# Three edits to a two-layer streaming encoder kernel: an enforced order of the out-projection's products, a sum's base load on GpSimd's queue, and the final norm's buffers in the tiles of the X sums

## The chip, the cores and the metric

The kernel runs on one core of a Trainium2 chip. A core has a matrix engine (TensorE, PE in the rows; its weight loads are PEld), a vector engine (VectorE, DVE), a scalar engine (ScalarE, ACT), a general engine (GpSimd, POOL) and SyncE (SP), which here only issues transfers. Each engine works through its own queue in order and waits there for semaphores of the others. SP and GpSimd both issue loads from the chip's memory; loads that add to what is already in the tile are issued by GpSimd here. The metric is the device time of one execution in microseconds (us), the median of several runs.

## The reference

One inference step of a two-layer encoder on 640 frames (512 of a new stream, 8 x 16 of running streams), with 1024 features, in float32:

```
def swiglu_ffn(h, g, w_in, w_out):
    a, b = jnp.split(rms_norm(h, g) @ w_in, 2, axis=-1)
    return h + (jax.nn.silu(a) * b) @ w_out
...
for l in range(DEPTH):          # DEPTH = 2
    if l < N_A_LAYERS:          # layer 0
        h, st = conv_module(h, conv_hist[l], ...)
    else:                       # layer 1
        h = h + o @ w_o[j]      # o: chunked band attention over a shared K and V
    h = swiglu_ffn(h, norm_ffn[l], w_ffn_in[l], w_ffn_out[l])
return rms_norm(h, norm_final), jnp.stack(new_hist, axis=0), k, v
```

The hidden width of the FFN is 2816, so w_in is 1024 x 5632 and w_out 2816 x 1024. The change lies in the two FFNs and in the last line's norm.

## The kernel before

The residual stream `h` stays on the chip as 8 tiles of 128 features by 640 frames. A float32 product is made of three TensorE products of split operands: each operand is cut into a high part (ACT copies it, rounded) and a low part (DVE subtracts the high one), and high x high, low x high and high x low are summed in one bank of PSUM. `cut` does this for weights (line 319 for ACT, 320 for DVE), `product` (line 383) issues the three matmuls of each 128-row step.

**The FFN** multiplies blocks in the manner of Strassen: the 640 frames are halved into 2 x 320 columns and the contraction into two halves, and seven products of sums replace eight plain ones. The sums of the normed input are kept for the whole FFN in tiles `XH0` to `XH6` and `XL0` to `XL6` (high and low parts of X11, X21, XT2, XT1, XT3, XT4, X22). The weight side needs its own sums for each block; `w_seven` makes them. It loads the block of four quarters into one of two `raw` tiles and the third quarter into one of two sum tiles `s1`, both from SP, and then adds the fourth quarter to `s1` with an adding load from GpSimd (line 365). DVE makes the other sums (lines 369, 370, 372), and each of the seven goes through `cut` into one of eleven weight slots that are used in turn: a slot is free when TensorE has done the product eleven places before.

The in-projection runs over 22 tiles of hidden features, 18 of them in three chunks of six. `seven` issues the products of one such tile (84 matmuls); the last two of them are handed on as `after(0)` and `after(1)` and issued within the next tile. Their sinks make the gated hidden values and their Strassen sums, again as high and low parts (tiles `hid`).

After each chunk `out_chunk` adds the chunk's part of the out-projection: four blocks u = 0 to 3, seven products each (63 matmuls), each product followed by an add of its PSUM bank to `h` on DVE (line 512). `QORD` names the order: the first digit is the product (5 XT1, 1 X11, 2 X21, 6 XT2, 3 X22, 7 XT3, 4 XT4), the second the block, and a0 and a1 are the last in-projection tile's `after(0)` and `after(1)`. The hidden sums of that tile come out of a0 and a1 alone, so the third 128-row step of products 6, 3, 7 and 4 can't begin before a1's residue is through ACT and DVE. The program is written in this order, but the order on each engine is set by a scheduler that weighs priorities against a timeline of its own; it may place matmuls of several products between one another, as long as the data allow it.

The last four hidden tiles are handled without block sums: `mm3` (lines 167 to 169) multiplies them by w_out for all 8 output tiles, first for frames 256 to 639, then for frames 0 to 255, and DVE adds each result to `h` (line 621).

**The final norm** follows for the same two groups of frames, g = 1 (384 frames) and g = 0 (256). `rstd_bc` squares the 8 tiles of `h` on ACT (line 175), sums the squares on DVE (line 194), takes the mean over partitions on TensorE (line 203), adds epsilon on DVE (line 237), raises to -0.5 on GpSimd (line 244) and spreads the result over the partitions on TensorE (line 215). Then the tiles of `h` are scaled, for g = 1 four on DVE (line 1216) and four on ACT and GpSimd (lines 1219, 1221), for g = 0 all on DVE, and stored from SP. The squares go through a new pool `tp3` with two tiles, and the sum and the copy `b1` of the spread lie in that pool too.

## Time and profile before

| | us |
| --- | --- |
| median of 3 runs | 1525.98 (1524.56 to 1526.48) |
| profiled execution | 1530.94 |
| its span, first to last instruction | 1528.9 |
| mean granted TensorE clock | 0.980 of full speed |

The first FFN lies at about 255 to 672 us of the span, the second at about 1048 to 1505 us, the final norm behind it. Times in rows are us from the span's start, durations of one instruction in ns or us as said there. In the rows a name stands for a tile, `out<-in`; buffer numbers are left out, so `s` is a sum tile `s1`, `w` the PSUM tile of a norm, `whi`, `wlo`, `shi` and `slo` weight slots. A bracket at the end of a timeline row gives how long the engine sat idle before it and what ended that. A matmul's end is modelled, so two matmuls that follow each other without a pause overlap in the rows; how full TensorE is, is better read from the number of matmuls in a stretch.

### The profile page before, as it was taken

The numbers are of one execution on the slowest core, as the hardware profiler recorded it, in microseconds if no ns is written. First come the engines' busy times: TensorE is split into PE (matmuls) and PEld (weight loads), VectorE is DVE, ScalarE is ACT, GpSimd is POOL, SyncE is SP. The second block draws the span as 40 slices with busy tenths as digits, with TensorE's granted clock in tenths as the row PEclk, the third lists the DMA queues.
The fourth block names the chain that finished last, engine by engine and source line by source line (L and its number), as shares of the span: only waits on it lengthen the run. The fifth ranks groups of instructions, "written<-read, shape, count | busy, mean of one in ns | idle before, by whom it ended". The sixth has DMA issues, their size and how long they took to land.

```text
span 1528.9 us, 28150 instructions
## 1 busy us (share of the span) xinstructions
PE 1456.1 (95%) x10974; PEld 1378.4 (90%) x10974; DVE 1120.0 (73%) x2481; ACT 746.7 (49%) x1617; POOL 281.8 (18%) x312
## 2 busy tenths in 40 slices
PE   5999899999999999999999999988999999999995
PEld 5998689999999999999887888957999999999994
DVE  5789346798888887856676667653799788688844
ACT  3666245464554563545554454442465464464432
POOL 5789232000000000013221121011000001001001
PEclk9999889999999999999999999988999999999997
DMA  7267414134444444424555455551124543444501
GB/s 236 65 185 182 102 48 132 44 101 117 149 116 126 139 116 132 111 83 149 193 188 189 138 173 187 168 166 42 56 76 111 158 127 93 143 138 92 169 29 69
DMA packets 71013, 192.57 MB, mean 126 GB/s; under 512 B 12000, under 2 KB 33248, under 8 KB 62432
## 3 DMA queue, kind: packets, MB, share of 16 engines
q1 hardware_dynamic: 61664, 175.78, 35.7%
q0 software_dynamic: 8928, 14.68, 6.4%
q8 instruction: 86, 1.41, 0.4%
q10 hardware_dynamic: 288, 0.31, 0.1%
q14 instruction: 47, 0.39, 0.1%
HBM read 179.14 MB, written 11.61 MB: 125 GB/s over the span
## 4 chain that ended last, share of the span: by engine, by line
PE 77%; DVE 8%; POOL 5%; DMA 5%; ACT 3%; issue 2%; SPq 0%; POOLq 0%; DVEq 0%; ACTq 0%
PE mm L383 44%; PE mm L167 7%; PE mm L168 7%; PE mm L169 7%; POOL ca L730 4%; PE mm L768 2%; DMA raw<-in_w_in 1%; PE w L1105 1%; PE w L203 1%; PE am L1090 1%; DVE wlo L320 1%; DMA cache<-in_ck 1%; PE am L1073 1%; PE am L1136 1%; DMA s<-in_w_in 1%
## 5 line engine op out<-in xcount | busy, mean ns | idle before, releaser
L383 PE MATMUL mm<-XH,whi 128*128 128x320 f32 x896 | 275.8, 310 | 4.5 <-DVE t L397 3.0
L383 PE MATMUL mm<-XH,wlo 128*128 128x320 f32 x896 | 276.5, 310 | 0.0
L383 PE MATMUL mm<-XL,whi 128*128 128x320 f32 x896 | 273.8, 309 | 0.0
L319 ACT ACTIVATE whi<-raw 128x512 fp32r<-128x512 f32 (+2 forms) x280 | 166.3, 612 | 156.7 <-PE mm L383 90.5
L167 PE MATMUL mm<-xh,whi 128*128 128x320 f32 (+2 forms) x640 | 202.0, 317 | 4.6 <-ACT xh L156 2.6
L168 PE MATMUL mm<-xh,wlo 128*128 128x320 f32 (+2 forms) x640 | 201.2, 315 | 0.6 <-DVE wlo L151 0.6
L169 PE MATMUL mm<-xl,whi 128*128 128x320 f32 (+2 forms) x640 | 198.1, 314 | 0.0
L320 DVE TENSOR_TENSOR wlo<-raw,whi 128x512 fp32r<-128x512 f32 (+2 forms) x280 | 183.6, 670 | 14.1 <-ACT whi L319 12.7
L383 PE MATMUL mm<-hid,whi 128*128 128x320 f32 x732 | 172.2, 309 | 2.6 <-ACT whi L319 2.3
L383 PEld LDWEIGHTS mm<-XH,whi 128*128 128x128 f32 x896 | 167.8, 188 | 6.5 <-DVE t L397 3.5
L383 PEld LDWEIGHTS mm<-XH,wlo 128*128 128x128 f32 x896 | 168.2, 188 | 0.5 <-DVE wlo L320 0.5
L383 PEld LDWEIGHTS mm<-XL,whi 128*128 128x128 f32 x896 | 167.6, 188 | 0.0
L167 PEld LDWEIGHTS mm<-xh,whi 128*128 128x128 f32 x640 | 122.5, 192 | 8.1 <-ACT xh L156 3.1
L383 PEld LDWEIGHTS mm<-hid,whi 128*128 128x128 f32 x732 | 124.9, 188 | 4.0 <-ACT whi L319 3.4
L365 POOL DMA_DIRECT2D s<-in_w_in x38 | 33.8, 890 | 503.9 <-DVE XL L320 115.7
L168 PEld LDWEIGHTS mm<-xh,wlo 128*128 128x128 f32 x640 | 122.7, 192 | 1.2 <-DVE wlo L151 0.8
L169 PEld LDWEIGHTS mm<-xl,whi 128*128 128x128 f32 x640 | 121.5, 191 | 1.2 <-issue 1.0
L383 PE MATMUL mm<-hid,wlo 128*128 128x320 f32 x366 | 112.5, 308 | 0.0
L383 PE MATMUL mm<-XL,shi 128*128 128x320 f32 x344 | 105.4, 308 | 1.3 <-DVE XL L320 1.3
L383 PE MATMUL mm<-XH,shi 128*128 128x320 f32 x344 | 106.0, 308 | 0.4 <-ACT XH L319 0.4
L383 PE MATMUL mm<-XH,slo 128*128 128x320 f32 x344 | 106.0, 308 | 0.1
L319 ACT ACTIVATE shi<-raw 128x512 fp32r<-128x512 f32 (+1 forms) x114 | 66.4, 587 | 73.5 <-PE mm L383 38.6
(229 smaller groups left out, 3368.7 us busy)
## 6 DMA issues: line engine op xcount, KB each, us to landing
raw<-in_w_in SPq DMA_DIRECT2D x38, 1024.0 KB
raw<-in_w_os SPq DMA_DIRECT2D x24, 768.0 KB
cache<-in_ck SPq DMA_DIRECT2D x32, 512.0 KB
cache<-in_cv SPq DMA_DIRECT2D x32, 512.0 KB
raw<-in_w_pw SPq DMA_DIRECT2D x12, 1024.0 KB
s<-in_w_in SPq DMA_DIRECT2D x38, 256.0 KB
s<-in_w_in POOLq DMA_DIRECT2D x38, 256.0 KB, 4.8
raw<-in_w_kq SPq DMA_DIRECT2D x8, 1024.0 KB
```

Of the source, the lines that this page charges most:

```text
L167: nc.tensor.matmul(ps, wh, xh, start=(i == 0), stop=False)
L168: nc.tensor.matmul(ps, wl, xh, start=False, stop=False)
L169: nc.tensor.matmul(ps, wh, xl, start=False, stop=(i == last))
L203: nc.tensor.matmul(st[:, 512 + t * w + k:513 + t * w + k], s[:, a:a + P], onec, start=True, stop=True)
L319: nc.scalar.activation(out=hi, in_=src, func=AF.Copy)
L320: nc.vector.tensor_tensor(out=lo, in0=src, in1=hi.bitcast(F32), op=sub)
L365: nc.gpsimd.dma_start(s1, src[:, 3 * n:4 * n], accum_op=add)
L383: nc.tensor.matmul(pt, wt, v, start=(first and k == i == 0), stop=(k == len(xs) - 1 and i == 2), skip_group_check=True)
L730: nc.gpsimd.tensor_tensor(out=acc, in0=acc, in1=pr, op=ALU.add)
L768: nc.tensor.matmul(pt[32 * q:32 * q + 32, 0:n], w4[0:r, 4 * tg + q, :], mv, start=(tg == 0), stop=(tg == 7))
L1073: nc.tensor.transpose(tr[:, o:o + P], S[:, SOFF[i] + k * P:SOFF[i] + (k + 1) * P], ident)
L1090: nc.tensor.matmul(po[r, k * P:512], VT[:, 1 + k, v0:v0 + DH], PTs[hh][:, POFF[k]:POFF[k] + n], start=(k == 0), stop=(k == 3))
```

## The change

Three edits:

1. In `out_chunk` each product is issued after the last matmul of the one named before it in `QORD` (`issue_after`), a0 and a1 included. This binds the scheduler's order and puts no wait into the program, since all of it is on one engine. Products 60 and 30 are written in two parts: the first two 128-row steps (60', 30') and the third (60", 30").
2. In `w_seven` the base of the sum tile, the third quarter, is loaded from GpSimd's queue instead of SP's, at the priority of the adding load.
3. The final norm's squares, sums and `b1` get no pool of their own. `ffn` hands back `spare`, which takes the tiles `XH0` to `XH6` again: for g = 1 the squares and the sum lie in XH0 to XH2 and `b1` in XH3, for g = 0 in XH4 to XH6.

```diff
@@ -58,7 +58,8 @@
 X11, X21, XT2, XT1, XT3, XT4, X22 = range(7)
 NCH, CW = 3, 6
 HIX = {X11: 0, X21: 1, XT1: 2, XT2: 3, XT3: 4, X22: 5, XT4: 6}
-QORD = "50 a0 10 a1 20 51 11 60 30 21 70 61 31 40 52 71 12 22 41 62 32 53 72 13 23 42 63 33"
+QORD = """50 a0 10 a1 20 60' 30' 51 60" 11 30" 70 21 61 40 31 52 71 12 22 41 62 32 53 72 13 23 42 63
+          33"""
 BO = "a0 s0 a1 s1 b0 b1 t0 p0 c0 t1 c1"
 BL = "a0 s0 a1 s1 t0 b0 b1 c0 t1 c1 p0"
 SSQ1 = 'ppapappp'
@@ -231,7 +232,7 @@
                 accp=None, sqs=None):
         st = w2t()
         nt = len(tiles(n))
-        r, v = colmean(st, [lambda s=s, e=e, i=i: square(s, n, e, sqs if sqs is None else sqs[:, i, :])
+        r, v = colmean(st, [lambda s=s, e=e, i=i: square(s, n, e, sqs and sqs[i])
                          for i, (s, e) in enumerate(zip(pieces, engs))], n,
                        cut, "rst", eng, accp)
         nc.vector.tensor_scalar(out=r[:, :nt], in0=v, scalar1=EPS, scalar2=None,
@@ -358,10 +359,10 @@
             n = src.shape[-1] // 4
             raw, ws = wraw(), {}
             s1 = wx.tile([P, 512], F32, tag="s1", name=nm("s1"))[:, :n]
-            nc.sync.dma_start(s1, src[:, 2 * n:3 * n])
             nc.sync.dma_start(raw[:, :4 * n], src)
             a12, a11, a21, a22 = (raw[:, n * i:n * i + n] for i in range(4))
             with tc.high_priority(offset=HP):
+                nc.gpsimd.dma_start(s1, src[:, 2 * n:3 * n])
                 nc.gpsimd.dma_start(s1, src[:, 3 * n:4 * n], accum_op=add)
                 for x in ((XT1, X11, X21, XT2, X22, XT3, XT4) if out else
                           (X11, X21, XT2, XT1, XT3, XT4, X22)):
@@ -375,16 +376,19 @@
                                  XT4: a22}[x])
             return ws
 
-        def product(pt, w, xs, first, o=0):
+        def product(pt, w, xs, first, ks=None):
             (hi, lo), o0 = w
-            for k, (xh, xl) in enumerate(xs):
+            n = len(xs)
+            for k in ks or range(n):
+                xh, xl = xs[k]
                 c = slice(o0 + k * P, o0 + k * P + P)
                 for i, (wt, v) in enumerate(((hi[:, c], xh), (lo[:, c], xh), (hi[:, c], xl))):
-                    nc.tensor.matmul(pt, wt, v, start=(first and k == i == 0),
-                                     stop=(k == len(xs) - 1 and i == 2), skip_group_check=True)
+                    last = nc.tensor.matmul(pt, wt, v, start=(first and k == i == 0),
+                                            stop=(k == n - 1 and i == 2), skip_group_check=True)
+            return last
 
         def xproduct(pt, w, x, first):
-            product(pt, w, [(XH[x][:, k, :], XL[x][:, k, :]) for k in range(4)], first)
+            return product(pt, w, [(XH[x][:, k, :], XL[x][:, k, :]) for k in range(4)], first)
 
         def keep(tag, pt):
             t = tp.tile([P, NH], F32, tag=tag, name=nm(tag))
@@ -481,13 +485,14 @@
 
             def after(i):
                 if i == 0:
-                    xproduct(pa, ws[XT4], XT4, False)
+                    last = xproduct(pa, ws[XT4], XT4, False)
                     sink(0, t1, pa)
                 else:
-                    xproduct(pe, ws[X22], X22, False)
+                    last = xproduct(pe, ws[X22], X22, False)
                     plus(t2, pe)
                     silu(t2, t2)
                     sink(1, t2, t3)
+                return last
 
             return after
 
@@ -498,7 +503,7 @@
                     3: ("e", X22, False, 1, 0), 7: ("a", XT3, False, 1, 1),
                     4: ("a", XT4, False, 0, 1)}
 
-            def go(i, u):
+            def go(i, u, part):
                 if u not in ws:
                     o = (4 * c + u) * 12 * P
                     ws[u] = w_seven(w_os[:, o:o + 12 * P], True)
@@ -506,17 +511,24 @@
                 if first:
                     pts[b, u] = mmt()[:, :NH]
                 pt = pts[b, u]
-                product(pt, ws[u][x], list(zip(HH[x], HL[x])), first)
+                with tc.issue_after(last[0]) if last else nullcontext():
+                    ins = product(pt, ws[u][x], list(zip(HH[x], HL[x])), first,
+                                  {"": None, "'": (0, 1), '"': (2,)}[part])
+                last[:] = [ins.ins]
+                if part == "'":
+                    return
                 hv = h[:, 2 * u + row, half * NH:half * NH + NH]
                 with tc.high_priority(offset=HP):
                     nc.vector.tensor_tensor(out=hv, in0=hv, in1=pt, op=sub if row else add)
 
+            last = []
             for t in QORD.split():
                 if t[0] == "a":
-                    after(int(t[1]))
+                    with tc.issue_after(last[0]):
+                        last[:] = [after(int(t[1])).ins]
                 else:
-                    go(int(t[0]), int(t[1]))
-            return lambda i: go((7, 4)[i], 3)
+                    go(int(t[0]), int(t[1]), t[2:])
+            return lambda i: go((7, 4)[i], 3, "")
 
         def stats(half):
             bc, _ = rstd_bc([h[:, k, half * NH:half * NH + NH] for k in range(KT)], NH, SQ, 6, None,
@@ -622,6 +634,12 @@
                                             in1=h[:, m, g0:g0 + n], op=add)
         hs.close()
 
+        def spare(i):
+            t = xo.tile([P, 4, NH], F32, name=nm("spare"), tag=f"XH{i}")
+            return t.rearrange("p a n -> p (a n)")
+
+        return spare
+
     cv = early
     cp = cv.enter_context(tc.tile_pool(name="cp", bufs=1))
 
@@ -782,7 +800,8 @@
             nc.vector.tensor_tensor(out=y[g][:, c, :], in0=y[g][:, c, :], in1=mu[:, :n],
                                     op=ALU.subtract)
         sq = xp.tile([P, KT, n], F32, tag="xl1", name=nm("sql"))
-        bc, _ = rstd_bc([y[g][:, c, :] for c in order], n, SQ, SQCUT[g], sqs=sq)
+        bc, _ = rstd_bc([y[g][:, c, :] for c in order], n, SQ, SQCUT[g],
+                        sqs=[sq[:, i, :] for i in range(KT)])
         z = new_xs(g)
         with tc.high_priority(offset=HP * (1 - g)):
             for c in range(KT):
@@ -1198,16 +1217,17 @@
     early.close()
 
     hf = ExitStack()
-    ffn(1, w_in1, w_out1, w_os1, ((256, 384), (0, 256)), hf)
-    tw[0] = 384
-    sqt[:] = "sq", "acc", 1
-    tp = hf.enter_context(tc.tile_pool(name="tp3", bufs=2, reuse_waits="tile"))
+    spare = ffn(1, w_in1, w_out1, w_os1, ((256, 384), (0, 256)), hf)
     bcs = {}
     with tc.high_priority(offset=HP):
         for g in (1, 0):
-            bcs[g], _ = rstd_bc([hp(g, k) for k in range(KT)], GR[g][1], SQ, KT, None, nc.vector)
+            n, (t0, t1, t2, t3) = GR[g][1], ([spare(i) for i in range(4)] if g else
+                                             [spare(i) for i in (4, 5, 6)] + [None])
+            sqs = [t[:, n * i:n * i + n] for t in (t0, t1, t2) for i in range(3)]
+            bcs[g], _ = rstd_bc([hp(g, k) for k in range(KT)], n, SQ, KT, None, nc.vector,
+                                accp=sqs[8], sqs=sqs)
             if g == 1:
-                b1 = tp.tile([P, 384], F32, tag="n1", name="b1", bufs=1)
+                b1 = t3[:, 0:384]
                 nc.scalar.activation(out=b1, in_=bcs[1], func=AF.Copy)
     for g in (1, 0):
         g0, n = GR[g]
```

How it moves instructions shows at three places.

TensorE, second out chunk of the first FFN: before, the stretch in which the first matmuls of block 2 come (mm_573 is its first product, 52, mm_574 its product 12; mm_551, mm_555 and mm_568, mm_569 belong to blocks 0 and 1):

```order
L383 MATMUL mm_555_5017<-hid_557_5045,whi_317_2795 128x320
L383 MATMUL mm_555_5017<-hid_557_5045,wlo_318_2796 128x320
L383 MATMUL mm_569_5107<-hid_557_5045,shi_325_2803 128x320
L383 MATMUL mm_569_5107<-hid_557_5045,slo_326_2804 128x320
L383 MATMUL mm_551_4988<-hid_560_5050,whi_319_2797 128x320
L383 MATMUL mm_568_5096<-hid_560_5050,whi_317_2795 128x320
L383 MATMUL mm_555_5017<-hid_558_5046,whi_317_2795 128x320
L383 MATMUL mm_569_5107<-hid_558_5046,shi_325_2803 128x320
L383 MATMUL mm_573_5211<-hid_490_4374,whi_317_2795 128x320
L383 MATMUL mm_574_5232<-hid_487_4339,whi_319_2797 128x320
L383 MATMUL mm_555_5017<-hid_508_4516,whi_319_2797 128x320
```

The same start of product 52 now:

```order
L386 MATMUL mm_568_5108<-hid_559_5049,whi_317_2795 128x320
L386 MATMUL mm_568_5108<-hid_559_5049,wlo_318_2796 128x320
L386 MATMUL mm_568_5108<-hid_560_5050,whi_317_2795 128x320
L386 MATMUL mm_573_5211<-hid_490_4374,whi_317_2795 128x320
L386 MATMUL mm_573_5211<-hid_490_4374,wlo_318_2796 128x320
```

Before, four products were issued one matmul at a time, and the first matmul of 52 stood 52 matmuls behind the last one of a1. Now whole products follow one another, that matmul stands 90 behind a1, and the third step of 60 (operand hid_557) has moved from 44 behind it to 30. On DVE, twelve instructions led from the add that begins a1's residue to the low part hid_558 before, nine do now; and between the release of the first tile's sum and the use of the third tile's, behind the second FFN's second out chunk, there are fourteen instead of eleven.

GpSimd's queue, the loads of the second FFN's blocks at the same place, before (adding loads alone):

```order
L365 DMA s1_1720_14580<-in_w_in1 128x512
L365 DMA s1_1728_14694<-in_w_in1 128x512
L365 DMA s1_1742_14827<-in_w_in1 128x512
L365 DMA s1_1762_14974<-in_w_in1 128x512
L365 DMA s1_1772_15103<-in_w_in1 128x512
```

and now (L365 is the base, L366 the adding load):

```order
L366 DMA s1_1720_14580<-in_w_in1 128x512
L365 DMA s1_1728_14694<-in_w_in1 128x512
L366 DMA s1_1728_14694<-in_w_in1 128x512
L365 DMA s1_1742_14827<-in_w_in1 128x512
L366 DMA s1_1742_14827<-in_w_in1 128x512
L365 DMA s1_1762_14974<-in_w_in1 128x512
```

Each base now stands directly ahead of its adding load, which waits for it; in the first out chunk of the first FFN two bases stand ahead of two adding loads.

DVE at the end of the program, before (L621 the residual adds, L194 the sums of squares):

```order
L621 TENSOR_TENSOR h_73<-mm_1882_16511,h_73 128x256
L621 TENSOR_TENSOR h_73<-mm_1883_16525,h_73 128x256
L621 TENSOR_TENSOR h_73<-mm_1884_16539,h_73 128x256
L194 TENSOR_TENSOR acc_1887_16560<-sq_1886_16558,sq_1888_16561 128x384
L194 TENSOR_TENSOR acc_1887_16560<-acc_1887_16560,sq_1889_16564 128x384
L194 TENSOR_TENSOR acc_1887_16560<-acc_1887_16560,sq_1890_16567 128x384
```

and now (L633 the adds, L195 the sums, L1236 the scalings):

```order
L195 TENSOR_TENSOR spare_1894_16587<-spare_1894_16587,spare_1893_16586 128x256
L633 TENSOR_TENSOR h_73<-mm_1882_16511,h_73 128x256
L1236 TENSOR_SCALAR h_73<-h_73,vec_76,w2_1889_16558 128x384 x4
L633 TENSOR_TENSOR h_73<-mm_1883_16525,h_73 128x256
L633 TENSOR_TENSOR h_73<-mm_1884_16539,h_73 128x256
L195 TENSOR_TENSOR spare_1894_16587<-spare_1894_16587 128x256 x2
L1236 TENSOR_SCALAR h_73<-h_73,vec_76,w2_1895_16588 128x256 x8
```

All sums stood behind the last add of the products; now all but the last two of them, and the scalings of the first group, stand among the adds. On TensorE the first group's mean now stands within the fourth product of the 256-column group and its spread ahead of the seventh.

2 lines of the change are left out of this document (1 added, 1 removed).

## The prediction

> **What bounds the kernel now.** I read the page first, then TensorE in stretches, then the timeline of the end.
>
> ```profile
> span 1528.9 us, 28150 instructions
> PE 1456.1 (95%) x10974; PEld 1378.4 (90%) x10974; DVE 1120.0 (73%) x2481; ACT 746.7 (49%) x1617; POOL 281.8 (18%) x312
> ...
> POOL 5789232000000000013221121011000001001001
> ...
> PE 77%; DVE 8%; POOL 5%; DMA 5%; ACT 3%; issue 2%; SPq 0%; POOLq 0%; DVEq 0%; ACTq 0%
> ```
>
> TensorE is busy for 95% of the span and holds 77% of the chain that ended last. No product is removed by the change, so what can be won is the time in which TensorE has none. Two kinds of it lie where the change works: short gaps inside the two FFNs, and the end of the program. Cut into pieces of 5 us, the FFNs are full nearly everywhere (36 matmuls, as at 420 us); of the pieces after each FFN's first products, thirteen fall short, six inside the out-projection chunks and seven around the chunks' ends and the blocks behind them. The first table below is of the six, the second of the seven (columns: stretch, length, TensorE busy and its matmuls, granted clock, DMA share, GB/s).
>
> ```profile
> 365.00:370.00 5.00, 4.42 (x30) 1.00 0.00 1
> 475.00:480.00 5.00, 4.41 (x31) 1.00 0.41 130
> ...
> 1400.00:1405.00 5.00, 4.41 (x31) 1.00 0.52 162
> sum 30.00, PE 26.60; mean PE 4.43
> ...
> 420.00:425.00 5.00, 5.00 (x36) 1.00 0.51 107
> ...
> 630.00:635.00 5.00, 4.12 (x29) 1.00 0.48 107
> ...
> 1330.00:1335.00 5.00, 3.27 (x22) 1.00 0.36 52
> sum 35.00, PE 30.70; mean PE 4.39
> ```
>
> The six lose 30.0 - 26.6 = 3.4 us, the seven 35.0 - 30.7 = 4.3 us: 7.7 us is all that the FFN parts of the change can win from gaps. The end is larger. The rows are of ACT, DVE, GpSimd and the chain of waits.
>
> ```profile
> 1504.52 0.52 ACT L175 ACTIVATE sq<-h 128x384 f32<-128x384 f32 x1 [15.94 <-PE mm L168]
> 1504.59 0.42 DVE L621 TENSOR_TENSOR h<-mm,h 128x256 f32<-128x256 f32 x1 [0.94 <-PE mm L169]
> 1515.78 0.41 ACT L175 ACTIVATE sq<-h 128x256 f32<-128x256 f32 x1
> 1515.92 2.19 DVE L1216 SCALAR_TENSOR_TENSOR h<-h,vec,w 128x384 f32<-128x384 f32 x4
> 1515.96 4.03 POOL L1221 TENSOR_TENSOR h<-h,b 128x384 f32<-128x384 f32 x4 [2.31 <-ACT b L1211]
> 1518.02 1.12 DVE L194 TENSOR_TENSOR acc<-acc,sq 128x256 f32<-128x256 f32 x1
> 1520.31 0.16 DVE L237 TENSOR_SCALAR rst<-w 128x2 f32<-128x2 f32 x1 [1.17 <-PE w L203]
> 1522.56 3.22 DVE L1216 SCALAR_TENSOR_TENSOR h<-h,vec,w 128x256 f32<-128x256 f32 x8 [2.09 <-PE w L215]
> ```
>
> The last residual add ends at 1504.59 + 0.42 = 1505.01. The final norm's second square waited 15.94 us, until TensorE's last product, though its input had been ready for long. So 16 squares, 14 sums and the means of both column groups stand behind the products: from 1505.01 to the last sum at 1518.02 + 1.12 = 1519.14 is 14.1 us. From there to the span's end it is 9.8 us (mean, power, spread, eight scalings, the last store).
>
> **The final norm's buffers.** The old pool tp3 lies where the hidden tiles were, which the last products read; the new squares lie in the X sums, whose last reader is the last seven-product block. No work is removed. In DVE's new queue the group of 384 columns is summed between the residual adds, and the group of 256 up to its sixth square. Behind the last add remain one square (0.41), one or two sums and their hand-overs. The nearest sums are
>
> ```profile
> 1512.50 0.41 DVE L194 TENSOR_TENSOR acc<-sq,sq 128x256 f32<-128x256 f32 x1
> ...
> 226.73 0.83 PE w L203 x6
> ...
> 195.64 0.86 PE w L215 x6
> ```
>
> 0.41 alone and 1.12 beside the GpSimd scalings of L1221. I take 1.2 us for what stays (bounds 0.9 and 2.1): 14.1 - 1.2 = 12.9 us go. Added ahead of the last product on TensorE are the mean and the spread of the first group, which now stand between products: 0.83 + 0.86 = 1.7 us by the two rows of the chain above, taken at full length (bound below: 0, if they are hidden in a gap; none is there). What hides the early norm work: DVE and ACT wait for TensorE between residual adds (0.94 us before each add of 256 columns in the row at 1504.59, 15.94 us on ACT). If that cover is gone, four scalings of 2.19 us in front of the last two adds delay them; in the new queue they stand there, while TensorE still has two products to do, so I count 0, with 0.9 us as the bound. Sum for the end: -12.9 + 1.7 = **-11.2 us**, bounds -12.6 and -9.4.
>
> At the end TensorE runs slower, too (two stretches, and the last spread in the chain):
>
> ```profile
> 1494.00:1504.00 10.00, 10.00 (x91) 1.00 0.01 2
> ...
> 1520.00:1524.00 4.00, 1.50 (x6) 0.50 0.58 210
> ...
> 1521.30 1.24 PE w L215 x4
> ```
>
> The clock is 0.50 when the last spread comes, and its four instructions take 1.24 us, against 0.86 for six at 195 us. I keep that price (inside the 9.8). The Trainium skill, TensorE: Matmul & The Clock Gate, section "What's actually happening", says that the clock halves after about 3.4 us of idling; by that rule TensorE would idle too briefly in the new order, and the last mean and spread would be about 0.6 to 1.1 us shorter. The sum by the rule is -12 us, by the row -11.2.
>
> **The enforced order.** It adds no instruction and no wait, only positions. In all six gaps of the first kind the same thing stands: around 479 us TensorE waits for ACT's split of the next block's sum.
>
> ```profile
> 478.61 0.53 ACT L319 ACTIVATE whi<-raw 128x384 fp32r<-128x384 f32 x1 [1.99 <-PE mm L383]
> 479.04 0.51 ACT L319 ACTIVATE whi<-s 128x384 fp32r<-128x384 f32 x1
> ...
> 479.60 0.44 PEld L383 LDWEIGHTS mm<-hid,whi 128*128 128x128 f32 x3 [0.85 <-ACT whi L319]
> ```
>
> ACT itself had waited 1.99 us for TensorE to give a weight slot back. The old queue has the first matmul of that product (mm_573) 52 matmuls behind the end of the chunk's a1, ahead of others whose operands are there; the new one has it 90 behind, 38 x 0.145 = 5.5 us later (0.145 = 5.0/34.5 from the full pieces). So these six gaps go: -3.4 us. What is late next is the split of the new hidden sums. In the old run the residue after a1 took, by DVE's rows, until the second hidden sum's low part
>
> ```profile
> 471.53 0.48 DVE L397 TENSOR_TENSOR t<-mm,t 128x320 f32<-128x320 f32 x1
> ...
> 476.73 0.48 DVE L320 TENSOR_TENSOR hid<-B,hid 128x320 fp32r<-128x320 f32 x1
> ```
>
> 5.7 us from a1's end. The new order asks for it 32 matmuls or 4.6 us behind a1; but DVE's new queue has nine instructions up to it instead of twelve, at 0.4 to 0.5 us each about 1.2 us less, 4.5 to 5 us. So 0 to 0.4 us is waited in each chunk, up to 1.1 if DVE keeps its old pace. I take 0.3 x 6 = +1.8, nearer to the shorter queue: -1.6 us for the order, bounds -3.4 and +3.2 (6 x 1.1 - 3.4).
>
> **The base load.** Nothing is removed: 38 loads leave SP's queue, and 38 more come to GpSimd's. SP's raw loads then no longer stand behind a load that waits for a sum tile. On GpSimd each costs 0.86 us of issue, in stages where the page's line of 40 slices shows it 0 or 1 tenths busy (slices 7 to 15 and 29 to 37). Who waits there is the second, adding load, queued behind its own base, and behind the base of the next block where that one goes first. The worst case of the old run, then DVE's waits for a sum in the first and the second FFN (us, times, longest), and the landing of GpSimd's loads in the first:
>
> ```profile
> 1318.59 0.33 SPq L361 DMA_DIRECT2D s<-in_w_in  x1
> ...
> 1322.20 0.86 POOL L365 DMA_DIRECT2D s<-in_w_in  x1 [23.68 <-DVE raw L369]
> ...
> 1329.98 0.69 DVE L370 TENSOR_TENSOR raw<-s,raw 128x512 f32<-128x512 f32 x1 [5.31 <-DMA s<-in_w_in]
> ...
> 1331.73 0.41 PE L383 MATMUL mm<-XH,whi 128*128 128x320 f32 x1 [2.14 <-DVE t L397]
> ...
> DVE raw L370 <- DMA s<-in_w_in: 6.7, 3, 4.3
> ...
> DVE raw L370 <- DMA s<-in_w_in: 7.5, 2, 5.3
> ...
> DMA to landing us min/median/max: 3.6/4.4/9.6
> ```
>
> The base took 1322.20 - 1318.59 = 3.6 us, the adding load until 1329.98; DVE stood 5.31 us, and TensorE 2.14 behind it. A base from GpSimd should take the median of its kin, 4.4 us: +0.8, up to +1.7 with the issue. The same sum would be later by that. Against it, the new order of DVE leaves three more instructions (11 becomes 14) between the release of that tile and the add, 1.4 us. I count 0 for the late sums, and a fifth of the seven gaps, -0.9 us, for raw loads that leave sooner: a fifth, because those gaps began with raw loads that waited for their own tile. Bounds: -4.3 (all seven gaps go) and +8.5 (the five waits each 1.7 us longer, all of it on TensorE).
>
> The Trainium skill, DMA: Bandwidth & Descriptors, section "Specifications", gives about 1 us to the first byte for loads from GpSimd and 0.6 for SP's; it speaks against this edit. By it each base is 0.4 us later and the sum 0.4 x 5 = 2 us worse at the most, if all waits of DVE for a sum grew; by the row it is +0.8 each, inside the bound above.
>
> **Sum.** -11.2 - 1.6 - 0.9 = -13.7 us. The profiled execution took 1530.94 us, 2.0 us of it outside the span of 1528.9; its span becomes 1515.2. The median of the runs, 1525.98, lies 5.0 us below it, and the same difference gives 1525.98 - 13.7 = 1512.3 us.
>
> **Rivals.** *The end alone.* The order opens as many waits as it closes and the late sums stay: for it speaks DVE at nearly full load in an out chunk, against it the 5.5 us that the blocked product gets. FFNs 0 to +4: 1515 to 1519, say 1516. *All gaps close*: the raw loads come sooner and the sums with them; -12 - 6.5: 1507.5. Against it, the late raw loads wait for their own buffers more than for a place in SP's queue. *The norm isn't overlapped*: the squares move, but DVE's and ACT's queues hold them up behind the adds until the products end, so that only ACT's waits for one of two square tiles are saved, 1526.0 - 2.6 = 1523.4.
>
> ```profile
> ACT sq L175 <- DVE acc L194: 2.6, 4, 1.6
> ```
>
>  Against it speaks that DVE's new queue has the sums between the adds. *Slower*: the chain base, landing, adding load, landing on one queue becomes the period of the blocks: 2 x (0.87 + 4.4) = 10.5 us against 9.1 us for a block of the out-projection (63 matmuls x 0.145). If the added 1.7 us reached TensorE in all 24 such blocks, +41 - 13.7: 1553. It decides from nine blocks on. Against it: with two sum tiles a chain has nearly two periods, and DVE waited for a sum in only 5 of 38 blocks.
>
> **How the numbers follow.** Forecast 0.55, end alone 0.22, all gaps 0.13, no overlap 0.05, slower 0.05. About 0.2% (3 us) is what a measurement can tell. Faster takes the first three and most of the fourth: 0.94; same 0.02; slower 0.04. The likeliest case with its bounds near the taken values gives 1508 to 1516; the end alone reaches to 1519, all gaps to 1505. The range 1505 to 1519 leaves out the last two cases and some of the edges.
>
> **What would show it.** In the new profile: the 384-column squares between the residual adds of that group, the last store some 11 us sooner behind the last residual add, with some 10 to 12 us between that add and the span's end instead of 24; full pieces (34 or more matmuls) in the middle of the out chunks; DVE's waits for a sum at 14 us in all or somewhat more. Wrong would be: a square that still waits for TensorE's last product; gaps of 1 us behind a1 in each chunk; or DVE waiting for sums in more than nine blocks.

## The result, and the profile after

| | before | changed |
| --- | --- | --- |
| median, nine runs each (us) | 1525.98 (1523.16 to 1529.14) | 1518.2 (1515.62 to 1522.07) |
| ratio of the times, with 95% interval | | 0.9951 (0.9938 to 0.9965) |
| profiled execution (us) | 1530.94 | 1522.07 |
| its span (us) | 1528.9 | 1520.3 |

The changed kernel is faster, by 7.8 us; 13.7 were forecast. The page of the changed kernel, the rows of the span and of the engines' busy time:

```profile
span 1520.3 us, 28089 instructions
PE 1455.1 (96%) x10974; PEld 1378.0 (91%) x10974; DVE 1129.3 (74%) x2481; ACT 755.8 (50%) x1617; POOL 318.6 (21%) x374
```

TensorE has the same 10974 matmuls and nearly the same busy time (1455.1 us after 1456.1). GpSimd has 62 instructions more (374 after 312), the moved loads.

**Where the time went.** The span can be cut at marks that every version has: a wait of TensorE for a part of the X sums at the start of each FFN (a low part in the first, a high part in the second), and the last residual add of each. The four rows of the changed kernel (timeline: start, duration, engine, line, operation, then in brackets the idle time before and what ended it):

```profile
269.80 0.41 PE L386 MATMUL mm<-XL,shi 128*128 128x320 f32 x1 [0.84 <-DVE XL L321]
...
695.74 0.56 DVE L633 TENSOR_TENSOR h<-mm,h 128x384 f32<-128x384 f32 x1
...
1081.36 0.42 PE L386 MATMUL mm<-XH,shi 128*128 128x320 f32 x1 [0.41 <-ACT XH L320]
...
1507.50 0.75 DVE L633 TENSOR_TENSOR h<-mm,h 128x256 f32<-128x256 f32 x2
```

| stretch (us) | before | changed | difference |
| --- | --- | --- | --- |
| first FFN (269.80 to 696.30) | 425.17 | 426.50 | +1.3 |
| between the FFNs (to 1081.36) | 385.00 | 385.06 | +0.1 |
| second FFN (to 1508.25) | 423.98 | 426.89 | +2.9 |
| behind the last residual add (to the end) | 23.89 | 12.05 | -11.8 |

By these marks the first FFN of the kernel before ends at 696.03 us, and not at about 672. The two FFNs and what follows them took 873.04 us before and 865.44 now, -7.6, close to the 7.8 us between the medians; the other 1.0 us by which the two spans differ lies ahead of the first mark and between the FFNs. The stretch between the FFNs has no part in the change, but between two executions of the changed kernel it differs by 5.5 us (385.06 and 379.51), so below the two FFNs and the end are summed for each kernel ("the three stretches"), and not whole spans. In the second execution of the changed kernel they sum to 865.81 us, 0.4 more than in the first.

**The end** did what was forecast, somewhat less of it:

```profile
1499.70 0.73 PE L204 MATMUL w<-onec,spare 128*128 128x1 f32 x6
1503.91 0.83 PE L216 MATMUL w<-ident,rst 128*128 128x128 f32 x6
1505.39 2.19 DVE L1236 SCALAR_TENSOR_TENSOR h<-h,vec,w 128x384 f32<-128x384 f32 x4
1505.44 3.90 POOL L1241 TENSOR_TENSOR h<-h,spare 128x384 f32<-128x384 f32 x4 [3.77 <-ACT spare L1231]
1508.40 1.75 DVE L195 TENSOR_TENSOR spare<-spare 128x256 f32<-128x256 f32 x2 [0.15 <-ACT spare L176]
1513.57 3.22 DVE L1236 SCALAR_TENSOR_TENSOR h<-h,vec,w 128x256 f32<-128x256 f32 x8 [2.09 <-PE w L216]
```

Mean and spread of the first group stand between the last products. Four scalings hold up the last two residual adds, which come as a pair at 1507.50. The last two sums take 1.75 us: the first, which begins while GpSimd still scales (until 1509.34), 1.22, and the second, behind that, 0.42. From the first add of the last products (1487.46 before, 1488.26 now) to the last one's end it is 2.4 us longer.

**The FFNs** traded one set of gaps for another. Of the pieces of 5 us below the first three are from the first FFN; the sum is of all twelve that fall short now. Behind them stand the first and the last of the seven that fell short around the chunks' ends before, and their sum:

```profile
345.00:350.00 5.00, 3.94 (x27) 1.00 0.52 73
...
360.00:365.00 5.00, 3.98 (x27) 1.00 0.48 157
460.00:465.00 5.00, 4.21 (x28) 1.00 0.65 147
...
sum 60.00, PE 50.32; mean PE 4.19
```

```profile
390.00:395.00 5.00, 5.00 (x37) 1.00 0.49 184
...
1330.00:1335.00 5.00, 5.00 (x36) 1.00 0.33 52
sum 35.00, PE 35.00; mean PE 5.00
```

All seven late gaps are gone, and so are the six waits for a weight split. But the out chunks now lose 60.0 - 50.3 = 9.7 us, all of it in waits for hidden sums (timeline of TensorE):

```profile
351.05 0.42 PE L386 MATMUL mm<-hid,whi 128*128 128x320 f32 x1 [2.10 <-ACT hid L320]
362.63 0.42 PE L386 MATMUL mm<-hid,shi 128*128 128x320 f32 x1 [1.02 <-DVE hid L321]
464.55 0.41 PE L386 MATMUL mm<-hid,whi 128*128 128x320 f32 x1 [0.80 <-ACT hid L320]
465.32 0.41 PE L386 MATMUL mm<-hid,whi 128*128 128x320 f32 x1 [0.21 <-DVE hid L321]
```

and, over the whole program, TensorE's waits by what they were for (us in all, times, longest):

```profile
PE mm L386 <- ACT hid L320: 6.6, 7, 2.1
PE mm L386 <- DVE hid L321: 3.1, 8, 1.0
```

In the order of the matmuls, the wait at 464.55 is at the third step of product **50**, the first of its chunk, ahead of a0; its operand is the XT1 sum of the in-projection tile before. That place costs 2.10 us in the first chunk and 1.0 in each of the other five, 7.15 in all. The wait at 362.63 is at the third step of 60, behind a1; that place costs 2.6 us, and does so in three of six chunks. The chain that ends at 464.55, on DVE and ACT:

```profile
460.68 0.48 DVE L401 TENSOR_TENSOR t<-mm,t 128x320 f32<-128x320 f32 x1
461.39 0.46 ACT L405 ACTIVATE t<-t 128x320 f32<-128x320 f32 x1
462.48 0.49 DVE L423 SCALAR_TENSOR_TENSOR B<-t,t 128x320 f32<-128x320 f32 x1
463.51 0.49 DVE L454 TENSOR_TENSOR B<-B,B 128x320 f32<-128x320 f32 x1
464.03 0.47 ACT L320 ACTIVATE hid<-B 128x320 fp32r<-128x320 f32 x1 [0.68 <-DVE B L454]
464.78 0.49 DVE L321 TENSOR_TENSOR hid<-B,hid 128x320 fp32r<-128x320 f32 x1
```

The residue of the tile before takes 4.6 us from its first add (460.68) to the end of the low part (465.27). The enforced order asks for the high part 0.8 us before it is there, and for the low part directly behind.

### The profile page after: what moved, and what is told of

It is laid out like the page before. It is cut to its first block, busy times and chain, and to the rows that moved or that the text cites. A ratio compares the mean times of both kernels' runs of the same rounds, so it can differ in the third digit from the quotient of the medians.

```text
span 1520.3 us, 28089 instructions
## 1 busy us (share of the span) xinstructions
PE 1455.1 (96%) x10974; PEld 1378.0 (91%) x10974; DVE 1129.3 (74%) x2481; ACT 755.8 (50%) x1617; POOL 318.6 (21%) x374
## 4 chain that ended last, share of the span: by engine, by line
PE 80%; DVE 7%; POOL 5%; DMA 3%; ACT 3%; issue 1%; SPq 0%; POOLq 0%; DVEq 0%; ACTq 0%
PE mm L386 47%; PE mm L168 8%; PE mm L169 7%; PE mm L170 7%; POOL ca L748 4%; PE mm L786 2%; PE w L1124 1%; PE w L204 1%; PE am L1109 1%; DMA cache<-in_ck 1%; PE am L1092 1%; PE am L1155 1%; DMA raw<-in_w_os 1%; DVE hid L540 1%; ACT whi L148 1%
## 5 line engine op out<-in xcount | busy, mean ns | idle before, releaser
L320 ACT ACTIVATE whi<-raw 128x512 fp32r<-128x512 f32 (+2 forms) x280 | 169.4, 614 | 150.6 <-PE mm L386 133.8
L365 POOL DMA_DIRECT2D s<-in_w_in x38 | 21.9, 577 | 392.4 <-DVE wlo L321 205.9
L748 POOL TENSOR_TENSOR ca<-ca,cvt 128x512 f32<-128x512 f32 x60 | 91.2, 1519 | 14.9 <-ACT cvt L745 8.0
```

Of the source, the lines that this page charges most:

```text
L320: nc.scalar.activation(out=hi, in_=src, func=AF.Copy)
L365: nc.gpsimd.dma_start(s1, src[:, 2 * n:3 * n])
L748: nc.gpsimd.tensor_tensor(out=acc, in0=acc, in1=pr, op=ALU.add)
```

## The experiments

### One edit at a time

Three kernels are the one before with one of the three edits each. The end alone (edit 3):

```diff
-    tp = hf.enter_context(tc.tile_pool(name="tp3", bufs=2, reuse_waits="tile"))
+    spare = ffn(1, w_in1, w_out1, w_os1, ((256, 384), (0, 256)), hf)
...
+            bcs[g], _ = rstd_bc([hp(g, k) for k in range(KT)], n, SQ, KT, None, nc.vector,
+                                accp=sqs[8], sqs=sqs)
```

> The kernel before with only the final norm's buffers moved (squares, sums and b1 in the tiles of the X sums; old order of the out-projection, base load on SyncE's queue). If the trace of the changed kernel is read rightly, this part alone is worth what its end shows: 11.85 us less behind the last residual add, 2.4 us more ahead of it, so -9.4 us, about 1516.6 us against 1526.0. By the forecast's own term it would be -11.2 us (1514.8). Rival: the end wins less by itself, because part of its overlap comes from the new order of the last chunk on DVE: -6 us or less. The FFN gaps of the kernel before (six of the first kind, 3.4 us in all; seven of the second, 4.3 us) should all still be there.

Measured: 1518.31 us against 1525.66, ratio 0.9940 (0.9919 to 0.9961), -9.2 us; the three stretches sum to 864.08, -9.0. (The ratio is the recorded one, and so is its interval; it is not the quotient of the two medians, which is 0.9952 here, or -7.4 us. Where a ratio is given, the difference is taken from it.) The rival falls: the overlap doesn't need the new order. The FFN gaps of before are there (the six took 3.4 us again, and among the late ones is a wait of 2.28 us for DVE).

Counted from the first add of the last products to the span's end, the end alone shows more than these sums: it took 41.44 us before, 32.04 in the changed kernel, 31.58 in that kernel's second execution and 29.97 here, which is -9.4, -9.9 and -11.5 us. The FFNs of this kernel, which no edit touches ahead of the last products, took 2.5 us longer than before. So a difference of 1 or 2 us in the FFNs of two single executions proves little; what the order does there is better read from the waits themselves.

The base load alone (edit 2):

```diff
-            nc.sync.dma_start(s1, src[:, 2 * n:3 * n])
             nc.sync.dma_start(raw[:, :4 * n], src)
...
+                nc.gpsimd.dma_start(s1, src[:, 2 * n:3 * n])
                 nc.gpsimd.dma_start(s1, src[:, 3 * n:4 * n], accum_op=add)
```

> The kernel before with only the base load of the block sum moved from SyncE's queue to GpSimd's. Theory A: the seven late gaps (4.3 us) closed because raw loads no longer stand behind base loads on SyncE's queue; then -4 us and those seven pieces full, the six others unchanged. Theory B: they closed because the enforced order frees weight slots and buffers on an even schedule; then this kernel is within 1 us of the kernel before and the seven gaps stay. The forecast's term was -0.9 us.

Measured: 1525.74 us against 1525.66, ratio 1.0000 (0.9982 to 1.0017); the three stretches 874.20, +1.2. Theory A falls: late gaps are there still, some in other places. From 300 to 660 and 1110 to 1470 us TensorE is without work for 6.9 us here and 7.7 in the kernel before.

```profile
380.00:385.00 5.00, 4.20 (x27) 1.00 0.64 243
...
390.00:395.00 5.00, 4.43 (x29) 1.00 0.20 26
...
630.00:635.00 5.00, 4.38 (x30) 1.00 0.36 88
```

DVE's waits for a sum tile grew, over the whole program, from 14.3 us in five waits before to

```profile
DVE raw L370 <- DMA s<-in_w_in: 16.8, 6, 4.6
```

so the sum does come somewhat later with the base on GpSimd's queue, and in the runs it makes no difference that shows; the interval, -2.7 to +2.6 us, is too wide to tell 0 from the forecast -0.9.

The enforced order alone (edit 1):

```diff
-QORD = "50 a0 10 a1 20 51 11 60 30 21 70 61 31 40 52 71 12 22 41 62 32 53 72 13 23 42 63 33"
+QORD = """50 a0 10 a1 20 60' 30' 51 60" 11 30" 70 21 61 40 31 52 71 12 22 41 62 32 53 72 13 23 42 63
+          33"""
...
+                with tc.issue_after(last[0]) if last else nullcontext():
```

> The kernel before with only the enforced order of the out-projection's products. In the changed kernel six new waits stand at the third step of product 50 (7.15 us in all, for the hidden sum of the tile before) and four at the third step of 60 (2.6 us), while the six old gaps (3.4 us) are gone. Theory A (late gaps closed by the base load): -3.4 + 9.75 = +6.3 us, with the seven late gaps still there. Theory B (closed by the order): +6.3 - 4.3 = +2 us, seven gaps gone. The forecast's term was -1.6 us.

Measured: 1530.71 us against 1525.66, ratio 1.0018 (0.9999 to 1.0038), +2.7 us (-0.2 to +5.8); the three stretches 873.99, +1.0. This is theory B: the seven pieces of the late gaps are full in this kernel, by their sum,

```profile
sum 35.00, PE 35.00; mean PE 5.00
```

and DVE never waits for a sum tile in it. It is the order that closes the late gaps, and gives back as much in waits for hidden sums: 7.8 us here, where 7.7 us of gaps are gone. Taken one by one, the parts give -9.2 + 0.0 + 2.7 = -6.5 us; together they gave -7.8, no difference by intervals of this width.

### Product 50 in two parts

```diff
-50 a0 10 a1 20 60' 30' 51 60" 11 30" 70 21 61 40 31 52 ...
+50' a0 10 50" a1 20 60' 30' 51 60" 11 30" 70 21 61 40 31 52 ...
```

> The changed kernel with one thing different: the third step of product 50 stands behind a0 and 10 in place of ahead of them (21 matmuls, about 3.0 us later). Theory: the enforced order loses 7.15 us there and only there is the wait; it goes, and little comes back at the third step of 60: -5 to -7 us against the changed kernel, 1511 to 1513 us. Rival: DVE's pace sets it, and the wait only moves on to the third step of 60: 0 to -2 us.

Measured: 1511.32 us against 1525.66, ratio 0.9907 (0.9878 to 0.9936), but over six runs alone; the three stretches 862.49, 2.9 less than the changed kernel. The median was partly luck: in a later set, with the end edited too, this order came 4.7 us ahead of the changed kernel beside it (the table below), and not 6.9. Both theories hold in part. At the third step of 50 the waits shrank from 7.15 us to 1.8, in two chunks; at the third step of 60 they grew from 2.6 us to 4.4, and came in five chunks of six, where DVE's low part is late:

```profile
474.40 0.41 PE L385 MATMUL mm<-hid,whi 128*128 128x320 f32 x1 [0.82 <-DVE hid L320]
```

### The third step of 60 behind 11

```diff
-50' a0 10 50" a1 20 60' 30' 51 60" 11 30" 70 21 ...
+50' a0 10 50" a1 20 60' 30' 51 11 60" 30" 70 21 ...
```

> As the kernel with product 50 split, and the third step of 60 moved behind 11 (9 matmuls, 1.3 us later). With 50 split, TensorE still waited 0.69 to 0.94 us once in each of the six chunks for DVE's low part of a hidden sum, five times at the third step of 60 (once, in the last chunk, also 1.09 us at 50), 6.5 us in all where the changed kernel has 9.75. Theory (the consumer is asked too early, DVE has time enough after it): about 4 us of it go: 1507 to 1508 us where the other gave 1511.3. Rival (DVE's pace is the limit and the wait goes to the next product that reads a new hidden sum, the third step of 30): 0 to -1 us against it.

Measured: 1521.29 us against 1526.83, ratio 0.9957 (0.9935 to 0.9978). A miss: no better than the changed kernel, and the three stretches, 868.16, are 5.7 us longer than with 50 alone split. Neither theory named the reason. The waits for hidden sums shrank to 1.6 us, and eight waits for DVE's adds to `h`, 9.7 us in all, took their place. The one at 473.83, with what DVE did ahead of it:

```profile
471.88 0.48 DVE L521 TENSOR_TENSOR h<-h,mm 128x320 f32<-128x320 f32 x1
472.35 0.56 DVE L320 TENSOR_TENSOR slo<-raw,shi 128x384 fp32r<-128x384 f32 x1
472.82 0.55 DVE L369 TENSOR_TENSOR raw<-raw 128x384 f32<-128x384 f32 x1
473.29 0.48 DVE L521 TENSOR_TENSOR h<-h,mm 128x320 f32<-128x320 f32 x1
473.83 0.42 PE L385 MATMUL mm<-hid,whi 128*128 128x320 f32 x1 [1.54 <-DVE h L521]
```

70 goes on adding to the PSUM tile that 60 has left, and may not touch it until DVE has added 60's result to `h`. With 60" moved back only the three matmuls of 30" lie between 60 and 70, and DVE has two pieces of weight work ahead of that add. A part of the loss is a lower clock behind two of these waits (last section).

The same order with the base load back on SyncE's queue (the base load's diff reversed):

> As the kernel with 50 and 60 split, but the base load of the block sum back on SyncE's queue. Theory (from the run with the base load alone, ratio 1.000): within 1 us of the kernel with 50 and 60 split. Rival: with the order enforced DVE's and ACT's work comes early enough for raw loads to be what is late, and the base load on SyncE costs 2 us or more.

Measured: 1520.29 us, ratio 0.9962 (0.9941 to 0.9983) against 0.9957 with the base load on GpSimd: no difference, as in the run of that edit alone. The base load is worth nothing that can be measured here, under either order.

### The end, with the scalings behind

This edit stands on the kernel with 60" behind 11 and the base load on GpSimd's queue.

```diff
-                nc.vector.scalar_tensor_tensor(out=hp(g, k), in0=hp(g, k), scalar=col(V_NFIN, k),
-                                               in1=bcs[g], op0=ALU.mult, op1=ALU.mult)
+                with tc.issue_after(rstop[0]) if g else nullcontext():
+                    nc.vector.scalar_tensor_tensor(out=hp(g, k), in0=hp(g, k),
+                                                   scalar=col(V_NFIN, k), in1=b1 if g else bcs[0],
+                                                   op0=ALU.mult, op1=ALU.mult)
```

`rstop` holds the second group's addition of epsilon. The scalings read `b1`, because both groups share one PSUM tile: while they read the spread from it, the second group's mean can't start, so in the changed kernel they have to stand ahead of it.

> As the kernel before this one, and at the end the four DVE scalings of the 384 columns stand behind the second group's addition of epsilon, and read the copy b1 in SBUF in place of the PSUM tile that both groups share. In the changed kernel they stand ahead of the last two residual adds (2.19 us at 1505.39), the last two adds then come as a pair of 0.75 us, and the last two sums take 1.75 us behind them. Theory: the span's end comes 1.0 us sooner (0.3 at the last add, 0.7 at the sums); the scalings hide in the 3.4 us in which DVE waits for mean, power and spread. Rival: the stores of the 384 columns, now behind these scalings, end the span: 0 to +1 us.

Measured: 1519.13 us, ratio 0.9956 (0.9933 to 0.9978), not to be told from the kernel without it (0.9957). In the trace the last add is single, and the last sum ends 1.76 us behind it (1.89 without the edit):

```profile
1504.65 0.41 DVE L634 TENSOR_TENSOR h<-mm,h 128x256 f32<-128x256 f32 x1
1505.55 1.27 DVE L194 TENSOR_TENSOR spare<-spare 128x256 f32<-128x256 f32 x1 [0.48 <-ACT spare L175]
1507.52 0.16 DVE L239 TENSOR_SCALAR rst<-w 128x2 f32<-128x2 f32 x1 [0.70 <-PE w L203]
1507.59 2.19 DVE L1238 SCALAR_TENSOR_TENSOR h<-h,vec,spare 128x384 f32<-128x384 f32 x4
1510.06 3.22 DVE L1238 SCALAR_TENSOR_TENSOR h<-h,vec,w 128x256 f32<-128x256 f32 x8 [0.27 <-PE w L215]
```

The scalings hide in the wait for the spread, which leaves 0.27 us of it. From the last add's end to the last scaling's end it is 8.22 us; in the kernel without the edit it was 8.53. The stores are not late: the span ends 3.4 us behind the last scaling, 3.5 without the edit. A gain of 0.6 us by the trace (31.43 us from the first add of the last products to the span's end, 32.04 without the edit), where 1.0 was expected.

### An order with room behind every producer

```diff
-50 a0 10 a1 20 60' 30' 51 60" 11 30" 70 21 61 40 31 52 71 ...
+50' a0 10 a1 50" 20 60' 30' 51 11 60" 30" 21 70 61 31 40 52 71 ...
```

This order alone, then with the edit of the end, then the order with 50 alone split and that end, and beside them the changed kernel itself, on one chip:

> The changed kernel with the order 50' a0 10 a1 50" 20 60' 30' 51 11 60" 30" 21 70 61 31 40 52 ...: the third step of 50 behind a1, the third step of 60 behind 11, and 21 put between 30" and 70. In the kernel with only 50 and 60 split the waits for hidden sums were 1.6 us in all, but TensorE waited 0.2 to 1.7 us at 70, eight times, 9.7 us in all, for DVE's residual add of 60, which reads the tile that 70 goes on adding to. Theory (each wait is one consumer placed too close behind its producer, and DVE has room): with 9 matmuls more between them the 70 waits shrink by 1.3 us each; 2 to 3 us of waits are left where the changed kernel has 9.75: about 7 us faster than the changed kernel on the same chip. Rival (DVE's pace in the first 20 us of a chunk is the limit, so any order waits as much): within 1.5 us of the changed kernel.

> The same order, with the end of the tail experiment (the four DVE scalings of the 384 columns behind the second group's epsilon, reading b1). By the trace of the tail experiment the end comes 0.6 us sooner (last add single, the sum for epsilon 0.5 us sooner, the power 0.3 us longer beside the scalings). Theory: 0.6 us faster than the same order without it; the rival that the stores become late: 0 to +1 us.

> The kernel with 50 alone split (its six waits were 6.4 us in all against 9.75 of the changed kernel), with the same end. Theory: 3.4 + 0.6 = 4 us faster than the changed kernel on the same chip; if its first median (ratio 0.9907 against before) holds, 7 us faster.

> The changed kernel itself, unedited, on the same chip as the three orders beside it, so that they can be set against it directly. Theory: ratio 0.995 to the kernel before again, 9.5 to 10 us of waits in the out-projection chunks.

| kernel | median (us) | ratio to before (1527.74) | three stretches (us) |
| --- | --- | --- | --- |
| changed kernel | 1520.03 | 0.9946 (0.9929 to 0.9964) | 865.81 |
| 50 split, end edited | 1515.32 | 0.9916 (0.9899 to 0.9933) | 859.67 |
| new order | 1511.28 | 0.9895 (0.9877 to 0.9914) | 856.82 |
| new order, end edited | 1510.28 | 0.9889 (0.9871 to 0.9906) | 855.00 |

The theory of room holds: by the medians 8.8 us faster than the changed kernel, where 7 were expected. The changed kernel repeated its ratio (0.9946 after 0.9951), with 9.2 us of waits for hidden sums where 9.5 to 10 were expected, and the order with 50 alone split came out 4.7 us faster than it, where 4 were expected. TensorE's busy time in 300 to 660 and 1110 to 1470 us, new order:

```profile
300.00:660.00 360.00, 356.77 (x2426) 1.00 0.44 121
1110.00:1470.00 360.00, 359.18 (x2439) 1.00 0.44 121
sum 720.00, PE 715.95; mean PE 357.98
```

4.0 us are left without work there, against 7.7 in the kernel before and 10.0 in the changed one; these 6.0 us are what the trace shows of the 8.8. The largest wait left is at 70 in the first chunk of the first FFN,

```profile
363.50 0.41 PE L385 MATMUL mm<-hid,whi 128*128 128x320 f32 x1 [1.87 <-DVE h L521]
```

and in the other five chunks no row shows a wait at 50, 60 or 70. The new order with the edited end beats both kernels, the one before by about 17 us; what the edited end adds to it (1.0 us in the medians, 1.8 in the three stretches, but only 0.1 from the first add of the last products to the span's end) lies within the intervals. DVE's pace, the rival, isn't what limited the other orders: the same DVE work fits when its consumers come later.

## Why the prediction was right, and where it was wrong

**The sign and most of the size** came from the end, as forecast: -9.4 us in the changed kernel (-11.8 behind the last add, +2.4 ahead of it), -9.2 (5.9 to 12.4 by the interval) for that edit alone, against -11.2 with bounds of -12.6 and -9.4. The lower bound doesn't follow from its own terms, which give 14.1 - 0.9 = 13.2 us gone and nothing added, -13.2. The mechanism was right in every step; in the changed kernel three sizes were off, and in the kernel with the end alone the same stretch came to -11.5, about the forecast, so a part of this lies in the execution. *What stays behind the last add* was taken as 1.2 us and is 1.9 (1508.25 to 1510.15), near its bound of 2.1: both last sums stand there, and the one beside GpSimd's scalings takes 1.22 us where 0.41 was the undisturbed price. *Ahead of the last add* 1.7 us were taken; mean and spread came to 0.73 + 0.83 = 1.56, as forecast, but 0.3 us go to the last two adds as a pair behind the four scalings, which were counted at 0 with a bound of 0.9, and 0.5 I can't assign. *From the last sum on* it is 10.15 us, not 9.8.

**The clock rule** (the Trainium skill, TensorE: Matmul & The Clock Gate) was set aside in favour of the row. TensorE idled 2.81 us ahead of the last mean, less than the 3.4 us that the Trainium skill names there (section "What's actually happening"), and still had half its clock behind it, with mean and spread at 0.98 and 1.22 us (stretch, length, TensorE's busy time and matmuls, granted clock, DMA share, GB/s):

```profile
1507.50:1510.20 2.70, 0.00 (x0) 1.00 1.00 359
1510.20:1514.00 3.80, 2.21 (x8) 0.50 0.42 156
```

In the kernel with the end alone the same 2.81 us of idling left a clock of 0.90, and the two took 0.58 and 0.71 us, 0.9 us less; there the price that the forecast had worked out from the Trainium skill came true:

```profile
1505.00 0.58 PE L203 MATMUL w<-onec,spare 128*128 128x1 f32 x4 [2.81 <-DVE spare L194]
1506.60 0.71 PE L215 MATMUL w<-ident,rst 128*128 128x128 f32 x4 [1.03 <-POOL rst L244]
```

Which of the two comes changes between executions. In the second execution of the changed kernel the mean took 0.58 us and the spread 1.23. Of the seven profiled executions with this end unedited, all with 2.80 or 2.81 us of idling, the mean took 0.98 us in three and 0.58 in four, and the spread 1.22 or 1.23 in all but the one with the end alone: the price of the row was the better one. The remark in the same section of the Trainium skill that the window of the clock gate is free-running agrees with the change from one execution to the next.

**The enforced order** was the step that failed. Forecast -1.6 us; alone it cost 2.7 by its runs (-0.2 to +5.8, which leaves out the forecast -1.6 but not 0) and 1.0 by the three stretches of one trace. "So these six gaps go: -3.4 us" is right. "What is late next is the split of the new hidden sums", asked for 32 matmuls behind a1, was right as well and costs 2.6 us where 1.8 was taken, though in three chunks and not in six. (The 0.145 us of a matmul there is not 5.0/36, by the full piece that is shown, but it agrees with matmuls that follow one another without a pause: in the changed kernel seven take 1.02 us from 267.63 us on.) What was not seen is that the enforced order asks for another new sum still sooner: all nine matmuls of 50 stand ahead of a0, and the third step reads the XT1 sum of the tile before. In four of the six chunks of the old order that step began 27 matmuls behind the product's first one; now it begins 6 behind it. This wait costs 7.15 us; putting the step behind 10 cut it to 1.8, and putting it behind a1 removed it. "It adds no instruction and no wait, only positions" hid it: only the places where an old wait had been were followed up, not each operand that came sooner.

**The base load**: -0.9 us forecast, 0.0 measured (-2.7 to +2.6). The term was given a fifth of the seven late gaps, for raw loads that would leave sooner. All seven went, but the order closed them, since they are gone in the kernel with the order alone; the base load alone leaves late gaps. So their 4.3 us belonged to the order's term, and with them it would have read -3.4 - 4.3 + 9.75 = +2.0, close to the +1.8 us that the FFNs came to in the changed kernel (-7.6 + 9.4), where -2.5 was forecast. The count of the moved loads was too small as well: 62, of which the 38 are the in-projection's. That the sums would be somewhat later from GpSimd's queue held in the kernel with the base load alone (14.3 to 16.8 us of DVE's waits), and no cost on TensorE showed. The 3.6 us that the forecast read for a base from SP's queue is only a bound: the row of the adding load names DVE, and not the landing of the base, as what ended its wait.

**The rivals.** What happened is the first one, the end alone: the order opens as many waits as it closes, FFNs 0 to +4, 1516. Its FFNs were right (+1.8); its end was the forecast's own, larger than in the changed kernel. The median, 1518.2, lies in the forecast range of 1505 to 1519 because that range was drawn wide enough for this rival; by the forecast's own terms it would have had to lie near 1512.3. The rival was held less likely because the blocked product 52 got 5.5 us more room, which is true and was not where the new wait came. The slow chain of loads on one queue did not show: DVE didn't wait for a sum at all in the changed kernel. Of the signs named beforehand, the squares between the adds and the 12 us behind the last add came; the full pieces in the out chunks did not, DVE's waits for a sum did not stay at 14 us but went to nothing, and the new gaps are ahead of a0 in all six chunks (1.0 to 2.1 us) and behind a1 in three (0.5 to 1.05 us).

## What to carry to other kernels

An order fixed by hand must be checked at every product for what became sooner, not only at the places that waited before: list for each product what its operands and its accumulator last wait for, and how many matmuls lie between. Here three kinds counted, a sum from the tile before, a sum from the tile just ended, and the accumulator that another engine must read first; mending one alone moved the wait to the next, and only the order that gave all three room paid in full. And work that can be taken out from behind the last product is worth its whole length, less what its pieces cost among the products.

## What the runs showed of the hardware

A wait of TensorE of some 1.7 us was at times followed by a lower granted clock, which costs nearly as much again as the wait. In the kernel with 60" behind 11 two of the waits of 1.7 us were followed by it and a third was not (columns: stretch, length, busy time and matmuls, granted clock, DMA share, GB/s):

```profile
1165.00:1170.00 5.00, 3.28 (x16) 0.83 0.26 109
...
1280.00:1285.00 5.00, 3.31 (x22) 1.00 0.24 100
1395.00:1400.00 5.00, 3.26 (x13) 0.70 0.11 45
```

In the 10 us from the start of each of these pieces 47 and 48 matmuls ran where the clock fell and 58 where it did not; 10 matmuls are 1.5 us at 0.145 us each. The length of a wait alone doesn't settle it: the one of 2.10 us in the changed kernel (at 351.05) was followed by a clock of 1.00, and one of 2.28 us in the kernel with the end alone by 0.66 (1325 to 1330 us).

In 1000 to 1060 us, which no edit touches, the granted clock was 0.83 in the changed kernel's profiled execution and 0.97 in the second one of the same kernel, and the stretch between the FFNs took 385.06 and 379.51 us. TensorE is idle there for some 2 us in 10; that the clock hangs on how these pauses fall is a guess that no run here tests. The spread of one kernel's runs (1515.62 to 1522.07 us) is of that size, and a difference of a few us between two spans says little until that stretch is taken out.
